# Sums of weight blocks in a Strassen MLP: VectorE adds or accumulating transfers

## The chip, the cores and the metric

The kernel runs on one core of a Trainium2 chip. The metric is the device time of one execution in microseconds. A core has TensorE (PE; matmuls), VectorE (DVE), ScalarE (ACT), GpSimd (POOL) and SyncE (SP), whose queue here only issues transfers. PE, DVE, ACT, POOL and SP each work through a row of instructions of their own, in order.

## What is computed

One residual block: a mixer sub-layer (a gated recurrence beside differential attention), then an MLP. Only the MLP is touched. It works on 512 positions of 1024 features, with 4096 hidden ones:

```python
h2 = rms_norm(x) * (1.0 + scale2) + shift2
ff = jnp.square(jax.nn.relu(h2 @ w_ff1[l])) @ w_ff2[l]
x = x + gate2 * ff
```

`scale2`, `shift2` and `gate2` come from a product with `w_ada` (adaLN).

## The kernel before

The numbers are float32. A matrix is split into a high and a low part (`wh`, `wl`; `p_0h`, `p_0l`): ACT casts the high part, DVE subtracts it to get the low one, and `mm3` (L131 to L133) multiplies high by high and high by low both ways, in three matmuls.

The MLP runs in four quarters (`qd` 0 to 3) of 1024 hidden features each. In a quarter, `hidden` computes eight blocks of 128 hidden features: each loads 512 KB of `w_ff1` (`load_w`, L120, three buffers with tag "w"), splits it (L124 on ACT, L125 on DVE, two buffers each) and runs 24 matmuls `f`, of 512 columns. In quarters 1 and 2 four of these blocks each also load a row of `w_ada` into a "w" buffer (L189) and reduce it on DVE (L190). Then `out_product` multiplies the quarter's 512 x 1024 activations by a 1024 x 1024 block of `w_ff2` with seven products p1 to p7, 24 matmuls each, in place of eight (Strassen's method). The weight side of four of them is a sum of 512 x 512 blocks b_00, b_01, b_10, b_11: p5 needs t1 = b_00 + b_01, p6 needs t2 = t1 + b_11, p7 needs t3 = b_01 + b_11, p4 needs t4 = t2 + b_10. Blocks are loaded in halves of 512 KB (`load_b`, L894, eight buffers with tag "b"), and each half is split like a weight (`split_b`, L940 and L941), 128 x 1024 elements per instruction. The halves are named `p_0` and `p_1` in the rows, whatever the product. Between the products, `beside()` runs the first three hidden blocks of the next quarter.

In quarters 0 to 2 the sums are made by `sums` (L984): DVE adds block onto block in place, so that the four blocks and all the sums take eight buffers. In quarter 3 (`by_dma`) they are made by transfers: `load_b` first loads one block into a buffer by a plain transfer on SP's queue (L894), then POOL issues transfers that add further blocks onto it (L896), and for t4 onto t2 (L917). Each accumulating transfer waits until the one before it on the same buffer has landed. That takes twelve half-block loads, so some of the eight buffers are used twice within the quarter.

The Tile scheduler sets the order of each engine's row from priorities and its own estimate of time; `tc.high_priority` moves the splits and the sums ahead. SP and POOL wait in order, so that a transfer whose buffer is not free holds up those behind it.

The functions that the change touches:

Of the kernel before, what the change touches and what calls it, by code (L numbers as in the profile page):

```python
# [21 lines left out]
ALU = mybir.AluOpType  # L22
# [20 lines left out]
HP = 130  # L43
# [10 lines left out]
def build(tc, out, x, xT_in, c, pos, vecs, reps, ada, w_xr, w_xr7, w_qk, w_v, w_gr, w_gm, w_lru,  # L54
          w_pr, w_pa, w_out, w_ff1, w_ff2):
    nc = tc.nc
    from contextlib import ExitStack

    with ExitStack() as es:
# [14 lines left out]
        def t_(name, dt=F32, tag="t"):  # L74
            return (tmp if tag == "t" else mix).tile([P, S], dt, name=name, tag=tag,
                                                     bufs=dict(t=B_T, a=B_A, r=B_R)[tag])
# [4 lines left out]
        def bank(name, tag="mm", bufs=4, dt=F32):  # L81
            return psum.tile([P, S], dt, name=name, tag=tag, bufs=bufs)
# [700 lines left out]
        acc = t_("acc", tag="a")  # L783
# [97 lines left out]
        def out_product(qd, raw, beside):  # L881
# [3 lines left out]
            def src_b(k, c, hf):  # L885
                k0 = (4 * k + 2 * hf) * P
                return w_ff2[qd, 4 * c:4 * c + 4, :, k0:k0 + 2 * P].rearrange("n p f -> p n f")

            def load_b(name, *parts):

                res = []
                for hf in range(2):
                    b = ff.tile([P, 4, 2 * P], F32, name=f"b{qd}_{name}{hf}", tag="b", bufs=8)
                    nc.sync.dma_start(b, src_b(*parts[0], hf))  # L894
                    for p_ in parts[1:]:
                        nc.gpsimd.dma_start(b, src_b(*p_, hf), accum_op=ALU.add)  # L896
                    res.append(b)
                return res

            def get_b(k, c):  # L900
                if (k, c) not in B:
                    B[k, c] = load_b(f"{k}{c}", (k, c))
                return B[k, c]

            by_dma = qd == 3

            def b_sum(name, acc, k, c, *parts):

                if not by_dma:
                    sums(acc, get_b(k, c))
                    return acc
                if acc is None:
                    return load_b(name, *parts, (k, c))
                for hf, b in enumerate(acc):
                    nc.gpsimd.dma_start(b, src_b(k, c, hf), accum_op=ALU.add)  # L917
                return acc
# [28 lines left out]
            def add_c(r, c, ps, sign):  # L947
                for t in range(2):
                    dst = C[r][c][t]
                    if qd == 0 and (r, c, t) not in seen:  # L950
                        seen.add((r, c, t))
                        nc.scalar.activation(dst, ps[t], AF.Copy, scale=float(sign))
                    else:
                        nc.vector.tensor_tensor(dst, dst, ps[t], op=ALU.add if sign > 0 else ALU.subtract)

            def product(name, a, bs, ps, first):

                fs = [split_b(b, f"{name}_{qd}_{i}", i) for i, b in enumerate(bs)]
                for hf in range(2):
                    for t in range(2):  # L960
                        for kk in range(2):
                            k = 2 * hf + kk
                            ts = slice(t * P, (t + 1) * P)
                            mm3(ps[t], a[0][:, k, ts], a[1][:, k, ts], fs[hf][0][:, kk], fs[hf][1][:, kk],
                                first and k == 0, k == 3, not first)
# [12 lines left out]
                                                   op0=ALU.mult, op1=ALU.add)  # L978
                    nc.sync.dma_start(out[n][:, cols], x1[n][:, cols])

            def sums(dsts, srcs):
                with tc.high_priority(HP):
                    for d, s_ in zip(dsts, srcs):
                        nc.vector.tensor_tensor(d, d, s_, op=ALU.add)  # L984

            X = [bank(f"X{qd}_{t}", "sc", 2) for t in range(2)]
            b11 = get_b(0, 0)
            product("p1", split_a(A[0][0], "a11", 2), b11, X, True)
# [7 lines left out]
            def second():  # L996
                a12 = split_a(A[0][1], "a12", 2)
                Y = [bank(f"Y{qd}_{t}") for t in range(2)]
                product("p2", a12, get_b(1, 0), Y, True)
                add_c(0, 0, Y, 1)  # L1000

            if qd == 3:
                second()
            t1 = b_sum("t1", None if by_dma else b11, 0, 1, (0, 0))
            Z = [bank(f"Z{qd}_{t}") for t in range(2)]
            product("p5", s1, t1, Z, True)
            beside()
            with tc.high_priority(HP):
                nc.vector.tensor_tensor(sx, sx, A[0][0], op=ALU.subtract)
                s2 = split_a(sx, "s2")  # L1010
            add_c(1, 1, Z, 1)
            t2 = b_sum("t2", None if by_dma else t1, 1, 1, (0, 0), (0, 1))
            product("p6", s2, t2, X, False)
            beside()
            with tc.high_priority(HP):
# [4 lines left out]
            nc.vector.tensor_tensor(A[0][0], A[0][0], A[1][0], op=ALU.subtract)  # L1020
            s3 = split_a(A[0][0], "s3")
            add_c(0, 1, Z, 1)
            t3 = b_sum("t3", None if by_dma else get_b(0, 1), 1, 1, (0, 1))
            product("p7", s3, t3, X, False)
            add_c(1, 1, X, -1)
            if qd < 3:
# [33 lines left out]
        for qd in range(4):  # L1060
            raw = hidden(qd, ahead)
            ahead = []

            def beside():

                if qd < 3:
                    ahead.append(t_(f"ahead{qd + 1}_{len(ahead)}"))
                    hidden_relu(qd + 1, len(ahead) - 1, ahead[-1])

            beside()  # L1070
            out_product(qd, raw, beside)
# [66 lines left out]
```

## Time and profile before

| | us |
|---|---|
| median of 3 runs (lowest, highest) | 875.87 (875.49, 876.06) |
| the profiled execution | 875.72 |
| its span, first to last instruction | 873.8 |
| PE busy | 860.9 (99%) |
| DVE busy | 636.8 (73%) |
| ACT busy | 478.6 (55%) |
| POOL busy | 15.1 (2%) |

The profile is of one execution. Its span starts at 0; the MLP's first matmuls run at about 540 us, and quarter 0's first product at 589 us. A busy PE is not the same as a PE at its best pace, since matmuls are pipelined: their starts tell the pace. Times to landing of a transfer run from its issue to the semaphore that tells of its end.

### The profile page before, as it was taken

Reading aid. Unit: us, or ns where it says so; the run is one execution under the profiler, and the core shown is the slowest. Engines: PE = TensorE matmul, PEld = TensorE weight load, DVE = VectorE, ACT = ScalarE, POOL = GpSimd, SP = SyncE. Lnnn points to the kernel's source line nnn. Section 1 sums busy time; section 2 is a strip of 40 time slices with the busy share of each in tenths; the row PEclk is TensorE's granted clock in tenths of the full one; section 3 lists DMA queues with packets and bytes.
Section 4 is the critical chain, followed back from the end, with each engine's and each line's share of the span. In section 5 each row is a group of like instructions: output and inputs, shape, how many; then the busy total and the mean of one; then the engine's idle time right before and its main releaser. Section 6 shows DMA issues by size and latency. Waiting matters only on the chain.

```text
span 873.8 us, 11279 instructions
## 1 busy us (share of the span) xinstructions
PE 860.9 (99%) x4012; PEld 706.1 (81%) x4012; DVE 636.8 (73%) x1155; ACT 478.6 (55%) x844; POOL 15.1 (2%) x50
## 2 busy tenths in 40 slices
PE   6999999999999999999999999999999999999998
PEld 3888887877878888888888888888888888888887
DVE  6998995699759754685657556858766885876397
ACT  6672547997538654646843343747545544554461
POOL 1000000000000000000000000000000000002110
PEclk9999999999999999999999999999999999999999
DMA  8979425512264372238445432822641345139572
GB/s 315 371 242 331 149 97 136 135 67 73 85 157 124 116 196 77 92 95 198 135 154 180 132 121 78 272 85 72 193 156 62 128 161 169 49 124 236 121 121 96
DMA packets 64571, 128.91 MB, mean 148 GB/s; under 512 B 6146, under 2 KB 30850, under 8 KB 64516
## 3 DMA queue, kind: packets, MB, share of 16 engines
q1 hardware_dynamic: 59236, 122.97, 44.6%
q0 software_dynamic: 5280, 5.24, 3.9%
q8 instruction: 31, 0.51, 0.2%
q14 instruction: 24, 0.20, 0.1%
HBM read 113.51 MB, written 2.10 MB: 132 GB/s over the span
## 4 chain that ended last, share of the span: by engine, by line
PE 92%; DVE 5%; ACT 1%; DMA 1%; issue 1%; SPq 0%
PE f L133 6%; PE f L131 6%; PE f L132 6%; PE X L132 3%; PE X L131 3%; PE X L133 3%; PE qk L133 3%; PE qk L131 3%; PE qk L132 3%; PE gm L132 2%; PE gm L131 2%; PE gm L133 2%; PE sc L582 2%; PE po L614 2%; PE xr L131 2%; PE v L131 2%
## 5 line engine op out<-in xcount | busy, mean ns | idle before, releaser
L124 ACT CAST wh<-w 128x1024 fp32r<-128x1024 f32 (+1 forms) x113 | 117.9, 1044 | 198.5 <-issue 44.9
L125 DVE TENSOR_TENSOR wl<-w,wh 128x1024 fp32r<-128x1024 f32 (+1 forms) x113 | 136.9, 1212 | 70.3 <-ACT wh L124 66.7
L133 PE MATMUL f<-h2h,wl 128*128 128x512 f32 x240 | 93.5, 390 | 0.4 <-DVE wl L125 0.4
L132 PE MATMUL f<-h2l,wh 128*128 128x512 f32 x240 | 93.2, 389 | 0.0
L131 PE MATMUL f<-h2h,wh 128*128 128x512 f32 x240 | 92.8, 390 | 0.0
L133 PEld LDWEIGHTS f<-h2h,wl 128*128 128x128 f32 x240 | 45.1, 188 | 10.1 <-DVE wl L125 0.8
L131 PEld LDWEIGHTS f<-h2h,wh 128*128 128x128 f32 x240 | 45.1, 188 | 9.4
L132 PEld LDWEIGHTS f<-h2l,wh 128*128 128x128 f32 x240 | 45.1, 188 | 9.2
L132 PE MATMUL gm<-hl,wh 128*128 128x512 f32 x128 | 51.7, 404 | 0.0
L133 PE MATMUL gm<-hh,wl 128*128 128x512 f32 x128 | 50.9, 398 | 0.0
L131 PE MATMUL gm<-hh,wh 128*128 128x512 f32 x128 | 50.7, 396 | 0.0
L131 PE MATMUL qk<-wh,hh 128*128 128x512 f32 x128 | 50.6, 396 | 0.0
L133 PE MATMUL qk<-wh,hl 128*128 128x512 f32 x128 | 50.5, 394 | 0.0
L132 PE MATMUL qk<-wl,hh 128*128 128x512 f32 x128 | 50.4, 394 | 0.0
L941 DVE TENSOR_TENSOR p_1l<-b,p_1h 128x1024 fp32r<-128x1024 f32 x24 | 29.3, 1222 | 26.3 <-ACT p_1h L940 26.1
L589 ACT ACTIVATE e<-e,nm 128x128 f32<-128x128 f32 (+3 forms) x64 | 35.5, 557 | 15.5 <-DVE nm L587 15.3
L940 ACT CAST p_1h<-b 128x1024 fp32r<-128x1024 f32 x24 | 25.2, 1051 | 31.0 <-PE f L132 22.9
L587 DVE CUSTOM_DVE_ANT_0 e<-sc,mask 128x128 f32<-128x128 f32 (+3 forms) x64 | 29.8, 484 | 16.1 <-PE sc L582 16.0
L941 DVE TENSOR_TENSOR p_0l<-b,p_0h 128x1024 fp32r<-128x1024 f32 x24 | 29.3, 1221 | 15.0 <-ACT p_0h L940 15.0
L940 ACT CAST p_0h<-b 128x1024 fp32r<-128x1024 f32 x24 | 25.3, 1055 | 24.6 <-PE X L133 12.4
L984 DVE TENSOR_TENSOR b<-b,b 128x1024 f32<-128x1024 f32 x24 | 29.0, 1217 | 0.1
L190 DVE CUSTOM_DVE_ANT_0 ada<-ada,cb,bada 128x1024 f32<-128x1024 f32 x16 | 20.5, 1282 | 10.1 <-DMA ada<-in_ada 10.1
(436 smaller groups left out, 2233.9 us busy)
## 6 DMA issues: line engine op xcount, KB each, us to landing
ada<-in_ada SPq DMA_DIRECT2D x64, 256.0 KB, 5.8
w<-in_w_ff SPq DMA_DIRECT2D x32, 512.0 KB, 3.3
b<-in_w_ff SPq DMA_DIRECT2D x30, 512.0 KB, 4.1
w<-in_w_qk SPq DMA_DIRECT2D x16, 512.0 KB, 3.3
w<-in_w_gm SPq DMA_DIRECT2D x16, 512.0 KB, 3.5
ada<-in_ada SPq DMA_DIRECT2D x16, 512.0 KB, 3.4
b_t<-in_w_ff POOLq DMA_DIRECT2D x10, 512.0 KB, 6.7
w<-in_w_gr SPq DMA_DIRECT2D x8, 512.0 KB, 3.6
```

The costliest lines, as they stand in the source:

```text
L124: i_w = nc.scalar.copy(wh[:, :n], w[:, :n])
L125: nc.vector.tensor_tensor(wl[:, :n], w[:, :n], f32(wh)[:, :n], op=ALU.subtract)
L131: nc.tensor.matmul(ps, lh, rh, start=first, stop=False, skip_group_check=more)
L132: nc.tensor.matmul(ps, lh, rl, start=False, stop=False, skip_group_check=more)
L133: nc.tensor.matmul(ps, ll, rh, start=False, stop=last, skip_group_check=more)
L190: nc.vector.tensor_tensor_reduce(w, w, cb, 1.0, bada[:, col:col + 1], op0=ALU.mult, op1=ALU.add, accum_out=mod[:, col:col + 1])
L582: nc.tensor.matmul(ps[m][:, :nn], q[m][:, qc], k[m][r][:, :nn], start=r == 0, stop=r == 1)
L587: nc.vector.tensor_tensor_reduce(e[:, :n], ps[m][:, :n], mask[:, S - n:], 1.0, 1e30, op0=ALU.add, op1=ALU.min, accum_out=nm)
L589: nc.scalar.activation(e[:, :n], e[:, :n], AF.Exp, bias=nm, scale=-1.0, accum_out=sums[:, 2 * i + m:2 * i + m + 1])
L940: nc.scalar.copy(v4(wh), v)
L941: nc.vector.tensor_tensor(v4(wl), v, f32(v4(wh)), op=ALU.subtract)
L984: nc.vector.tensor_tensor(d, d, s_, op=ALU.add)
```

## The change

The condition `by_dma` goes, and with it `sums`: all four quarters now make t1, t2, t3 and t4 by transfers, in the way of quarter 3. Quarter 3 itself is unchanged, and so is everything ahead of the MLP.

```diff
-            by_dma = qd == 3
-
             def b_sum(name, acc, k, c, *parts):
 
-                if not by_dma:
-                    sums(acc, get_b(k, c))
-                    return acc
                 if acc is None:
                     return load_b(name, *parts, (k, c))
                 for hf, b in enumerate(acc):
...
-            def sums(dsts, srcs):
-                with tc.high_priority(HP):
-                    for d, s_ in zip(dsts, srcs):
-                        nc.vector.tensor_tensor(d, d, s_, op=ALU.add)
...
-            t1 = b_sum("t1", None if by_dma else b11, 0, 1, (0, 0))
+            t1 = b_sum("t1", None, 0, 1, (0, 0))
...
-            t2 = b_sum("t2", None if by_dma else t1, 1, 1, (0, 0), (0, 1))
+            t2 = b_sum("t2", None, 1, 1, (0, 0), (0, 1))
...
-            t3 = b_sum("t3", None if by_dma else get_b(0, 1), 1, 1, (0, 1))
+            t3 = b_sum("t3", None, 1, 1, (0, 1))
```

The rows of PE stand in the same order as before. On the other engines the order moves. In what follows, `b_000` is the first half of block b_00, `b_t` a half of t1, t2 or t3, and the four-digit numbers tell buffers apart.

DVE, at the turn from quarter 0 to quarter 1, before:

```order
L954 TENSOR_TENSOR C_5557<-C_5557,Y_1_6098 128x512
L984 TENSOR_TENSOR b_000_6394<-b_000_6394,b_010_6447 128x1024
L125 TENSOR_TENSOR wl_6185<-w_6182,wh_6184 128x1024
L984 TENSOR_TENSOR b_010_6447<-b_010_6447,b_110_6527 128x1024
L941 TENSOR_TENSOR p_1_0l<-b_000_6394,p_1_0h 128x1024
L984 TENSOR_TENSOR b_000_6394<-b_000_6394,b_110_6527 128x1024
L125 TENSOR_TENSOR wl_6218<-w_6215,wh_6217 128x1024
L190 ISA ada_6284,mod<-ada_6284,cb,bada 128x1024
L190 ISA mod 128x1
L125 TENSOR_TENSOR wl_6254<-w_6251,wh_6253 128x1024
```

and now:

```order
L947 TENSOR_TENSOR C_5557<-C_5557,Y_1_6108 128x512
L125 TENSOR_TENSOR wl_6195<-w_6192,wh_6194 128x1024
L934 TENSOR_TENSOR p_1_0l<-b_t_6457,p_1_0h 128x1024
L190 ISA ada_6294,mod<-ada_6294,cb,bada 128x1024
L190 ISA mod 128x1
L125 TENSOR_TENSOR wl_6228<-w_6225,wh_6227 128x1024
L125 TENSOR_TENSOR wl_6264<-w_6261,wh_6263 128x1024
```

The three adds are gone, and the split of the fifth hidden block's weights (`wl_6218`, now `wl_6228`), which stood ahead of the reduction of the quarter's second adaLN row (`ada_6284`, now `ada_6294`), stands behind it. Quarter 2 has the same two in the same new order.

SP, in quarter 1, before:

```order
L894 DMA b_010_6447<-in_w_ff 128x4x256
L894 DMA b_011_6449<-in_w_ff 128x4x256
L894 DMA b_110_6527<-in_w_ff 128x4x256
L894 DMA b_111_6529<-in_w_ff 128x4x256
L894 DMA b_100_6688<-in_w_ff 128x4x256
L894 DMA b_101_6690<-in_w_ff 128x4x256
L189 DMA ada_6284<-in_ada 128x1024
L120 DMA w_6287<-in_w_ff 128x1024
```

and now:

```order
L894 DMA b_t_6457<-in_w_ff 128x4x256
L894 DMA b_t_6460<-in_w_ff 128x4x256
L894 DMA b_t_6537<-in_w_ff 128x4x256
L894 DMA b_t_6541<-in_w_ff 128x4x256
L894 DMA b_110_6617<-in_w_ff 128x4x256
L894 DMA b_111_6619<-in_w_ff 128x4x256
L894 DMA b_t_6660<-in_w_ff 128x4x256
L189 DMA ada_6294<-in_ada 128x1024
L894 DMA b_t_6663<-in_w_ff 128x4x256
L120 DMA w_6297<-in_w_ff 128x1024
```

Six loads of blocks have become eight; the second adaLN row's load stands behind the load of t3's first half, and the load of t3's second half stands ahead of the next weight load.

POOL, quarters 0 and 1, now (before, POOL had no transfer ahead of quarter 3):

```order
L896 DMA b_t_5938<-in_w_ff 128x4x256
L896 DMA b_t_5942<-in_w_ff 128x4x256
L896 DMA b_t_5938<-in_w_ff 128x4x256
L896 DMA b_t_5942<-in_w_ff 128x4x256
L896 DMA b_t_6061<-in_w_ff 128x4x256
L896 DMA b_t_6064<-in_w_ff 128x4x256
L910 DMA b_t_5938<-in_w_ff 128x4x256
L910 DMA b_t_5942<-in_w_ff 128x4x256
L896 DMA b_t_6457<-in_w_ff 128x4x256
L896 DMA b_t_6460<-in_w_ff 128x4x256
L896 DMA b_t_6537<-in_w_ff 128x4x256 x2
L896 DMA b_t_6541<-in_w_ff 128x4x256 x2
```

In quarter 0 both halves of t2 (`b_t_5938`, `b_t_5942`) get their first addition before either gets its second; from quarter 1 on a half gets both in a row (`x2`), so that POOL waits for a landing between them. t4's additions (L910) stand ahead of the next quarter's t1.

## Rows read from the trace of the kernel before

**Rows 1.** The page, sections 1 and 4: busy us and share; the chain by engine.

```profile
PE 860.9 (99%) x4012; PEld 706.1 (81%) x4012; DVE 636.8 (73%) x1155; ACT 478.6 (55%) x844; POOL 15.1 (2%) x50
...
PE 92%; DVE 5%; ACT 1%; DMA 1%; issue 1%; SPq 0%
```

**Rows 2.** Stretches, 562.2 to 861.1 us: length, busy us by engine, clock, DMA share.

```profile
589.10:643.50 54.40, 54.40 (x242) 45.06 (x241) 43.24 (x44) 31.01 (x39) 0.00 (x0) 1.00 0.40 127
...
sum 298.90, PE 298.90 PEld 247.53 DVE 214.43 ACT 152.81 POOL 12.86; mean PE 42.70 PEld 35.36 DVE 30.63 ACT 21.83 POOL 1.84
```

**Rows 3.** Waits of TensorE, 540 to 861 us: total, times, longest.

```profile
PE f L133 <- DVE wl L125: 0.4, 1, 0.4
```

**Rows 4.** Timeline of TensorE near 562, 573, 644 us: start, us, instruction, idle before.

```profile
561.22 0.39 PE L131 MATMUL f<-h2h,wh 128*128 128x512 f32 x1
561.45 0.39 PE L132 MATMUL f<-h2l,wh 128*128 128x512 f32 x1
562.20 0.50 PE L133 MATMUL f<-h2h,wl 128*128 128x512 f32 x1 [0.36 <-DVE wl L125]
...
573.22 0.39 PE L133 MATMUL f<-h2h,wl 128*128 128x512 f32 x1
...
643.94 0.39 PE L133 MATMUL f<-h2h,wl 128*128 128x512 f32 x1
```

**Rows 5.** Line 984, the removed adds: ns min/median/max, first and last start.

```profile
L984 DVE TENSOR_TENSOR b<-b,b x24: 1212/1216/1226, 562.1 to 768.7; 128x1024 f32<-128x1024 f32 x24
```

**Rows 6.** Line 896, issues on POOL: ns min/median/max.

```profile
L896 POOL DMA_DIRECT2D b_t<-in_w_ff x8: 1264/1277/1412, 789.2 to 837.4; - x8
```

**Rows 7.** POOL's transfers issued at 789.19, 797.94, 799.62, 809.02, 843.43: last column, us to landing.

```profile
b_t<-in_w_ff POOLq DMA_DIRECT2D x1, 512.0 KB, 8.4
...
b_t<-in_w_ff POOLq DMA_DIRECT2D x1, 512.0 KB, 10.8
...
b_t<-in_w_ff POOLq DMA_DIRECT2D x1, 512.0 KB, 14.0
...
b_t<-in_w_ff POOLq DMA_DIRECT2D x1, 512.0 KB, 7.3
...
b_t<-in_w_ff POOLq DMA_DIRECT2D x1, 512.0 KB, 6.0
```

**Rows 8.** SP's transfers issued at 553.74, 554.83, 635.89, 790.18, 793.20, 798.35.

```profile
b<-in_w_ff SPq DMA_DIRECT2D x1, 512.0 KB, 6.3
...
b<-in_w_ff SPq DMA_DIRECT2D x1, 512.0 KB, 8.2
...
ada<-in_ada SPq DMA_DIRECT2D x1, 512.0 KB, 3.2
...
b_t<-in_w_ff SPq DMA_DIRECT2D x1, 512.0 KB, 7.2
...
b_t<-in_w_ff SPq DMA_DIRECT2D x1, 512.0 KB, 5.9
...
w<-in_w_ff SPq DMA_DIRECT2D x1, 512.0 KB, 8.2
```

**Rows 9.** Timeline of ACT, quarter 0: casts for t1's and t2's first halves.

```profile
564.88 1.05 ACT L940 CAST p_0h<-b 128x1024 fp32r<-128x1024 f32 x1
...
592.00 1.06 ACT L940 CAST p_0h<-b 128x1024 fp32r<-128x1024 f32 x1 [0.36 <-PE X L133]
```

**Rows 10.** Timeline of VectorE, quarter 0 and the start of quarter 1.

```profile
567.10 0.69 DVE L145 TENSOR_TENSOR a11l<-r,a11h 128x512 fp32r<-128x512 f32 x1
...
631.17 1.22 DVE L941 TENSOR_TENSOR p_0l<-b,p_0h 128x1024 fp32r<-128x1024 f32 x1 [1.20 <-ACT p_0h L940]
...
634.65 1.22 DVE L125 TENSOR_TENSOR wl<-w,wh 128x1024 fp32r<-128x1024 f32 x1
...
639.38 1.23 DVE L125 TENSOR_TENSOR wl<-w,wh 128x1024 fp32r<-128x1024 f32 x1
640.52 1.27 DVE L190 CUSTOM_DVE_ANT_0 ada<-ada,cb,bada 128x1024 f32<-128x1024 f32 x1
```

## The prediction

> **What bounds the kernel now.** The page's first section comes first: TensorE is busy for 860.9 of 873.8 us, VectorE for 636.8, and the chain of work that ended last runs 92% over TensorE [rows 1]. A busy share can hide a lagging engine, so the next view is the table of stretches over the MLP. In the stretch from 562.2 to 861.1 us TensorE is busy for 298.90 of 298.90 us at a granted clock of 1.00 (2.4 GHz) [rows 2]. The waits of TensorE between 540 and 861 us are one line: 0.4 us, once, for `wl` on VectorE [rows 3]. The matmuls around it show its price: starts are 0.23 us apart, then one comes 0.75 us after the last, at 562.20, which is 0.5 us lost [rows 4]. All 24 adds that the change removes lie between 562.1 and 768.7 us, and stand on VectorE beside this unbroken row of matmuls [rows 5]. The reader should see here that the MLP has 0.5 us to win on TensorE, and that the question is whether something new makes TensorE wait.
>
> **The change part by part.** The order of matmuls stays the same row by row. The sum is made against the profiled execution, 875.72 us: its span of 873.8 and 1.9 around it, beside a median of 875.87 (875.49 to 876.06).
>
> *Removed from VectorE:* 24 adds of 1.216 us, 29.2 us [rows 5]. They lie wholly beside TensorE's work. The one stall at 562.20 waits for a split whose place in VectorE's order has no removed add ahead of it, so it stays. Gain: 0; at most the 0.5 us.
>
> *Added transfers:* in each of quarters 0 to 2, four more plain 512 KB loads on SP's queue (12 instead of 8) and ten accumulating ones on POOL's. Plain loads that queue up land 1.5 us apart (553.74 + 6.3 = 560.0 and, two later, 554.83 + 8.2 = 563.0) [rows 8]; accumulating ones that queue up without company 2.7 us apart (799.62 + 14.0 = 813.6, 809.02 + 7.3 = 816.3) [rows 7]. A quarter with adaLN rows would then ask for 24 x 1.5 + 10 x 2.7 = 63 us of transfers, and it lasts 360 matmuls of 0.227 us, 81.6 us. The transfers fit on average; before, the DMA share there is 0.40 [rows 2]. What counts is when single ones land. POOL does nothing else, and its issues take 1.26 to 1.41 us [rows 6].
>
> *Place A, quarter 0, t1's first half.* It was the first of the adds, at 562.1 [rows 5]; now it is a plain load and then an accumulating one, and the cast `p_0h` that reads it stands in ACT's row ahead of the split of the weights for the hidden block that starts at 572.76. The plain load is the one ahead of that issued at 553.74, so it lands 1.5 us before 560.0, at 558.5. An accumulating transfer takes 6.0 us to land alone, 8.4 when it is first in POOL's queue and plain loads run beside it, 10.8 and 14.0 when it stands behind other accumulating ones [rows 7]. This one is first in its queue with four loads still under way, so I take 8.4: it lands at 566.9, where the cast now starts at 564.88 [rows 9]. The limit: the cast 1.05, then on VectorE its low half 1.14, two `a11l` of 0.6 and the split `wl` of 1.22 make 4.6 us [rows 9, 10], and the third matmul of the block, at 573.22 [rows 4], needs that `wl`; so it may land at 568.6. That leaves 1.7 us. Cost 0; with the ends 6.0 and 14.0 it is 0 and 4.0 us.
>
> A rule of the Trainium skill says less for the same transfer: "DMA: Bandwidth & Descriptors", section "Anatomy of one DMA — SWDGE (gpsimd) path", fits 2.0 us plus the bytes over 436 GB/s, an estimate of 3.2 us for 512 KB. The rows have 6.0 alone. By the page the half would land at 561.7 with 6.9 us to spare, by the rows at 566.9 with 1.7; the sum is 0 by either, and the rows decide how near it is.
>
> *Quarter 0, t2*, two accumulating transfers on each half. From 797.6 to 813.6 us three steps of the queue took 5.3 us each [rows 7]. So t1's second half lands at 572, t2's first pass at 577.5 and 583, its second at 588 and 593.5. The cast that reads the first of these starts at 592.00 now [rows 9], the other one later. Hidden, with 4 us to spare. t3 and t4 come later than that and are read later still.
>
> *Place B, quarters 1 and 2.* Here the order of VectorE changes. Before, the split `wl` for the fifth hidden block stood ahead of the reduction of the second adaLN row (L190); now it stands behind it. TensorE needs that split at 643.94 in quarter 1 [rows 4], so the reduction, 1.27 with 1.21 to the next, and the split, 1.23 [rows 10], must start by 641.45: that is the limit for the landing of the adaLN row. It is issued when the `wl` ahead is done: that one starts at 634.65 [rows 10] behind an add that is gone, so it ends at about 635.1 instead of 635.9. Alone the row landed 3.2 us after its issue [rows 8], which would be 638.3. A weight load on the same queue behind loads of `b` with accumulating transfers beside took 8.2 [rows 8], which would be 643.3, 1.85 us too late. Nearer to the case: the transfer ahead of it on SP's queue is t3's load, which needs the buffer that the split at 631.17 [rows 10] frees, so it is issued at 632.4; loads beside accumulating transfers landed 5.9 and 7.2 us after issue [rows 8], so it lands between 638.3 and 639.6, and the adaLN row 1.5 later, 639.8 to 641.1. In quarter 3 three accumulating transfers were issued in the 9.2 us ahead of that weight load, the last at 797.94; here t1's two and t2's first spread over 17 us, since POOL then waits for t2's first pass to land. I take 640.5, 0.9 us before the limit. Cost 0; ends 0 and 1.85 us, in each of quarters 1 and 2 (81.6 us later the same chain stands again).
>
> *Queues passed:* SP waits in order, and the load for t3's second half waits for p5's first split in quarters 1 and 2, with the next weight load behind it. That split ends by about 638, and the weight load's own buffer comes free only behind the `wl` that starts at 639.38 [rows 10], so that wait costs nothing. But this `wl` now ends near 643 instead of 640.6 by the working above, and the weight load and the third adaLN row go out then; at 8.2 they land at 651.2, the row's reduction, an `a11l` and the `wl` behind it take 3.0, and TensorE needs that `wl` two blocks after 643.94, at 654.8. Hidden by 0.6 us. On POOL t4's transfers wait for p6's splits and the next quarter's t1 stands behind them; t1's buffers come free later than that anyway. *Quarter 3 and the tail* keep their rows.
>
> Sum: 875.72 + 0 (adds) + 0 (A) + 0 (B twice) = 875.7, in the middle of the three runs before; with their spread I forecast 875.9.
>
> **The rivals.**
>
> *Slower: the adaLN row lands behind the new traffic (place B).* Plain and accumulating transfers take each other's time: a `b` load took 7.2 us where the adaLN row alone took 3.2 [rows 8]. The margin is 0.9 us in an estimate that adds three transfers, and the wait falls straight on TensorE, which has no slack to take it back: the blocks behind it follow without a gap. It decides once the row takes over 6.35 us from issue to landing. At 8.2 it gives 1.85 us twice, 879.4; with 10.8 for A in place of 8.4 another 0.7, 880.1. Against it: the accumulating transfers lie wider than in quarter 3, and quarter 3 already runs all of them with TensorE fully occupied. A stall of under 1.75 us in all, the part of it that no measurement tells, is likelier than the full one.
>
> *Faster: VectorE's 29.2 us matter.* This would need TensorE to wait for VectorE. The rows leave 0.5 us, so 875.2 is the best, and this lies within 0.2%. A gain beyond that would need a pace of matmuls under 0.227 us; nothing in the profile points to one.
>
> *The change does nothing of what it says.* The 24 adds are gone from VectorE's row and 30 transfers stand on POOL's, so only the accumulation could be cheaper than quarter 3 shows: 875.7.
>
> **How the numbers follow.** A measurement of this kernel tells 0.2%, 1.75 us, from no change. No stall: 0.55, 875.4 to 876.2. A stall of under 1.75 us in A and B together: 0.21, 876.2 to 877.6. More than that: 0.20, 877.6 to 880.1. Gain over 1.75 us: 0.04, 873.9. So faster 0.04, within 0.2% 0.76, slower 0.20. The range runs from 875.3 to 879.0: it takes in one full stall and half of the second, and leaves about 0.1 above and 0.06 below.
>
> **What would show it.** VectorE's busy time falls by about 29 us to 608. TensorE stays busy for the whole of 562 to 861 us, and its waits remain one line of 0.4. In quarter 0 the cast `p_0h` of t1 starts near 566.9 after a wait for a DMA on `b_t`; over 568.6 would show on the block that starts at 572.76. In quarters 1 and 2 the second adaLN row lands about 5.4 us after issue, and VectorE waits for it ahead of L190. The forecast is wrong if TensorE's waits name `wl` at about 644 and 725.5 us, or `wh` or `wl` at 572.8; each such wait is its own price, and their sum the difference in the span. If none is there and the time still moves, the pace of the matmuls has changed, which this account has not foreseen.

## The result and the profile after

| | before | after |
|---|---|---|
| median (lowest, highest), us | 875.96 (875.49, 876.22), 4 runs | 881.38 (878.57, 882.59), 4 runs |
| ratio, 95% interval | | 1.0058 [1.0046, 1.0071] |
| the profiled execution, us | 875.72 | 881.36 |
| its span, us | 873.8 | 879.4 |

The changed kernel is 0.6% slower, above the range of the prediction (875.3 to 879.0); the sign is that of its rival "slower". Its runs also lie 4.0 us apart, those of before 0.7.

The page of after, sections 1, 3 and 4: busy time, queues (packets, MB, share of 16 DMA engines), and the chain by engine.

```profile
PE 861.5 (98%) x4012; PEld 705.6 (80%) x4012; DVE 611.2 (69%) x1131; ACT 478.6 (54%) x844; POOL 53.6 (6%) x80
...
q1 hardware_dynamic: 65572, 129.26, 46.0%
q0 software_dynamic: 21120, 20.97, 15.4%
...
PE 82%; DVE 10%; DMA 3%; ACT 2%; issue 1%; SPq 1%; DVEq 0%; ACTq 0%
```

VectorE lost its 24 adds and 25.6 us of busy time against [rows 1]. The adds' durations sum to 29.2, which the prediction expected; instructions that follow each other there overlap a little (by 0.09 us at 640.52 in [rows 10]), so that an add fills less than its duration. TensorE's busy time is what it was. The chain, 92% TensorE before, now crosses to VectorE, ScalarE and transfers. The stretch from 562.2 to 861.1 us of after (columns as in [rows 2]):

```profile
562.20:861.10 298.90, 295.07 (x1299) 243.38 (x1298) 185.92 (x201) 152.36 (x191) 50.11 (x40) 1.00 0.86 203
```

TensorE is busy for 295.07 of 298.90 us at the same granted clock of 1.00, where it was busy throughout [rows 2]. So the matmuls have not slowed; TensorE waits. Its waits between 540 and 880 us in after (total, times, longest), against the one of 0.4 us in [rows 3]:

```profile
PE f L133 <- DVE wl L125: 2.6, 3, 1.3
PE f L131 <- ACT wh L124: 1.3, 1, 1.3
```

Where they stand is told by the same matmuls in both traces, since TensorE's row is the same. After:

```profile
562.61 0.50 PE L133 MATMUL f<-h2h,wl 128*128 128x512 f32 x1 [0.37 <-DVE wl L125]
...
574.59 0.50 PE L131 MATMUL f<-h2h,wh 128*128 128x512 f32 x1 [1.26 <-ACT wh L124]
574.92 0.40 PE L132 MATMUL f<-h2l,wh 128*128 128x512 f32 x1
576.21 0.50 PE L133 MATMUL f<-h2h,wl 128*128 128x512 f32 x1 [0.89 <-DVE wl L125]
576.54 0.40 PE L131 MATMUL f<-h2h,wh 128*128 128x512 f32 x1
...
730.14 0.50 PE L133 MATMUL f<-h2h,wl 128*128 128x512 f32 x1 [1.32 <-DVE wl L125]
730.48 0.40 PE L131 MATMUL f<-h2h,wh 128*128 128x512 f32 x1
...
875.24 0.28 PE L133 MATMUL pl<-a22h,pl_1l 128*128 128x256 f32 x1
```

and before, the partners of the lines at 576.54, 730.48 and 875.24:

```profile
573.44 0.39 PE L131 MATMUL f<-h2h,wh 128*128 128x512 f32 x1
...
725.76 0.39 PE L131 MATMUL f<-h2h,wh 128*128 128x512 f32 x1
...
870.42 0.28 PE L133 MATMUL pl<-a22h,pl_1l 128*128 128x256 f32 x1
```

After runs behind before by 0.41 us at 562 (ahead of the change), by 3.10 behind the first hidden block, by 4.72 behind the block in quarter 2, by 4.82 at the last matmul, and by 5.6 at the end of the span. The 5.6 us are thus 0.4 that were there already, **2.7 at place A**, **1.6 at place B of quarter 2**, 0.1 between, and 0.8 in the tail. Place B of quarter 1 cost nothing in this execution. A wait costs more than its idle time: the three new ones are idle for 3.47 us (1.26, 0.89, 1.32) and cost 4.3, some 0.3 more each.

Place A in after, first on ACT, then on VectorE:

```profile
571.50 1.05 ACT L933 CAST p_0h<-b_t 128x1024 fp32r<-128x1024 f32 x1 [6.12 <-DMA b_t<-in_w_ff]
...
573.50 1.04 ACT L124 CAST wh<-w 128x1024 fp32r<-128x1024 f32 x1
```

```profile
572.59 1.22 DVE L934 TENSOR_TENSOR p_0l<-b_t,p_0h 128x1024 fp32r<-128x1024 f32 x1 [8.48 <-ACT p_0h L933]
...
574.93 1.22 DVE L125 TENSOR_TENSOR wl<-w,wh 128x1024 fp32r<-128x1024 f32 x1
```

The cast of t1's first half, which started at 564.88 [rows 9], waits 6.12 us for the accumulating transfer. `wh` and `wl` of the next hidden block stand behind it on ACT and on VectorE, and TensorE waits for each in turn. Place B on VectorE in after, quarter 1 and quarter 2:

```profile
644.11 1.28 DVE L190 CUSTOM_DVE_ANT_0 ada<-ada,cb,bada 128x1024 f32<-128x1024 f32 x1 [3.15 <-DMA ada<-in_ada]
...
645.32 1.22 DVE L125 TENSOR_TENSOR wl<-w,wh 128x1024 fp32r<-128x1024 f32 x1
...
727.65 1.28 DVE L190 CUSTOM_DVE_ANT_0 ada<-ada,cb,bada 128x1024 f32<-128x1024 f32 x1 [3.90 <-DMA ada<-in_ada]
...
728.86 2.36 DVE L125 TENSOR_TENSOR wl<-w,wh 128x1024 fp32r<-128x1024 f32 x2
```

In both, VectorE waits for the adaLN row with a split behind it. The transfers that all this hangs on, issued at 560.95 (t1's first half), 638.26 and 719.86 (the rows); the last column is us to landing:

```profile
b_t<-in_w_ff POOLq DMA_DIRECT2D x1, 512.0 KB, 10.5
...
ada<-in_ada SPq DMA_DIRECT2D x1, 512.0 KB, 5.7
...
ada<-in_ada SPq DMA_DIRECT2D x1, 512.0 KB, 7.7
```

### The profile page after: what moved, and what is told of

It is laid out like the page before. It is cut to its first block, busy times and chain, and to the rows that moved or that the text cites. A ratio compares the mean times of both kernels' runs of the same rounds, so it can differ in the third digit from the quotient of the medians.

```text
span 879.4 us, 11373 instructions
## 1 busy us (share of the span) xinstructions
PE 861.5 (98%) x4012; PEld 705.6 (80%) x4012; DVE 611.2 (69%) x1131; ACT 478.6 (54%) x844; POOL 53.6 (6%) x80
## 3 DMA queue, kind: packets, MB, share of 16 engines
q1 hardware_dynamic: 65572, 129.26, 46.0%
q0 software_dynamic: 21120, 20.97, 15.4%
## 4 chain that ended last, share of the span: by engine, by line
PE 82%; DVE 10%; DMA 3%; ACT 2%; issue 1%; SPq 1%; DVEq 0%; ACTq 0%
PE f L133 5%; PE f L131 5%; PE f L132 5%; PE X L132 3%; PE X L131 3%; PE X L133 3%; PE gm L132 2%; PE gm L131 2%; PE gm L133 2%; DVE wl L125 2%; PE qk L133 2%; PE qk L131 2%; PE qk L132 2%; DMA b_t<-in_w_ff 2%; PE sc L582 2%; PE po L614 2%
## 5 line engine op out<-in xcount | busy, mean ns | idle before, releaser
L896 POOL DMA_DIRECT2D b_t<-in_w_ff x32 | 41.2, 1500 | 719.3 <-DMA b_t<-in_w_ff 673.7
L934 DVE TENSOR_TENSOR p_0l<-b_t,p_0h 128x1024 fp32r<-128x1024 f32 x15 | 18.3, 1222 | 18.4 <-ACT p_0h L933 18.4
L133 PEld LDWEIGHTS qk<-wh,hl 128*128 128x128 f32 x128 | 24.1, 188 | 4.7
L132 PEld LDWEIGHTS qk<-wl,hh 128*128 128x128 f32 x128 | 24.1, 189 | 4.6
L131 PEld LDWEIGHTS qk<-wh,hh 128*128 128x128 f32 x128 | 24.2, 189 | 4.5
```

Source lines behind the costliest of these rows:

```text
L131: nc.tensor.matmul(ps, lh, rh, start=first, stop=False, skip_group_check=more)
L132: nc.tensor.matmul(ps, lh, rl, start=False, stop=False, skip_group_check=more)
L133: nc.tensor.matmul(ps, ll, rh, start=False, stop=last, skip_group_check=more)
L934: nc.vector.tensor_tensor(v4(wl), v, f32(v4(wh)), op=ALU.subtract)
```

## The experiments

Three groups of runs shared their runs of before: medians 875.85 (21 runs), 876.10 (33) and 876.07 (26). Each result is the median of 5 to 11 runs and the ratio to before with its interval.

**By quarter.** Sums by transfers in quarter 0 alone (`q0_only`) or in quarters 1 and 2 alone (`q12_only`), beside quarter 3; the rest by `sums` as before.

```diff
-            by_dma = qd == 3
+            by_dma = qd in (0, 3)
...
-            by_dma = qd == 3
+            by_dma = qd > 0
```

> Sums by transfers in quarter 0 (and, as before, in quarter 3); quarters 1 and 2 keep VectorE's adds, and VectorE's row there is that of before. Theory (two places: A, t1's first half lands too late in quarter 0; B, the split of the fifth hidden block waits behind the second adaLN row in quarters 1 and 2): A stays, about 2.5 us lost at the hidden block that starts near 573 us, B is gone; with 0.4 to 0.8 us that I have not placed, 878.4 to 879.3. Rival (30 more transfers slow everything a little, a third in each of three quarters): 5.4 / 3 = 1.8, so 877.8, and no single stall of over 1 us.

> Sums by transfers in quarters 1, 2 and 3; quarter 0 keeps VectorE's adds. Theory of the two places: no wait at 573 us; a wait of TensorE for wl at the fifth hidden block of quarter 2 (near 726 us) and perhaps of quarter 1 (near 644), 0 to 2 us each, its size that of the adaLN row's landing over 6.35 us; about 877.4, between 876 and 879. Rival (a little everywhere): 879.5.

Measured: 876.79, 1.0012 [1.0003, 1.0021], and 877.72, 1.0030 [1.0018, 1.0042]. The two add up to 2.8 of 5.4 us. What makes the other 2.6 is not settled: the profiled execution of after lost 2.4 us more at A than that of `q0_only`, and 0.4 more in the tail than both together, but a profile is one execution of each kernel. "A little everywhere" falls for `q12_only`: TensorE waits there for `wl` at one place of quarter 2 and nowhere else beyond the old 0.4.

```profile
726.39 0.50 PE L133 MATMUL f<-h2h,wl 128*128 128x512 f32 x1 [1.03 <-DVE wl L125]
```

For `q0_only` my number was too high. Its profiled execution, the fastest of its eleven, loses only 0.3 us at A: the accumulating transfer is as slow as in after (10.2 us), but it was issued at 558.00, not at 560.95, since the plain load that POOL waits for landed 3 us sooner (the semaphore of its landing is complete at 557.12, in after at 560.08). Only 0.9 of that is the earlier MLP (the old stall of 562.61 stands at 561.70 there). The same cast as above:

```profile
568.20 1.05 ACT L938 CAST p_0h<-b_t 128x1024 fp32r<-128x1024 f32 x1 [3.72 <-DMA b_t<-in_w_ff]
```

So place A costs from 0.3 to 2.7 us in the two executions that were profiled. The median of `q0_only` is 0.9 above before, and 0.3 of that can be its tail (3.7 us from the last matmul to the end, 3.4 before). That the runs of these kernels lie further apart than those of before fits this, though the slower runs themselves left no trace to see it in.

**A alone taken away.** All sums by transfers but t1 of quarter 0 (`t1_q0_dve`).

```diff
-            t1 = b_sum("t1", None, 0, 1, (0, 0))
+            if qd == 0:
+                t1 = b11
+                sums(t1, get_b(0, 1))
+            else:
+                t1 = b_sum("t1", None, 0, 1, (0, 0))
```

> The changed kernel, but t1 of quarter 0 alone is made by two adds of VectorE, as before; all other sums by transfers. Theory of the two places: A is gone (no wait at 573 us), B stays as in the changed kernel: 878 to 879.3. If t2's first pass, which is now first in POOL's queue, were also late, a wait would show near 592 us or later. Rival (a little everywhere): 28 of 30 transfers are left, 881.

Measured: 879.11, 1.0040 [1.0028, 1.0052], 2.3 us under after, though the two intervals overlap. What the trace shows is that the wait at 573 is gone. Two waits for `wl` are left:

```profile
661.10 0.50 PE L133 MATMUL f<-h2h,wl 128*128 128x512 f32 x1 [0.96 <-DVE wl L125]
...
727.69 0.50 PE L133 MATMUL f<-h2h,wl 128*128 128x512 f32 x1 [0.99 <-DVE wl L125]
```

The second is place B in quarter 2. The first is one that no theory named: place C, the fourth adaLN row of quarter 1, again with a split behind its reduction. That order is not new: in before the reductions of the third and fourth rows already stand ahead of their splits, as here the fourth and its split:

```profile
652.03 1.29 DVE L190 CUSTOM_DVE_ANT_0 ada<-ada,cb,bada 128x1024 f32<-128x1024 f32 x1 [0.82 <-DMA ada<-in_ada]
...
655.42 1.23 DVE L125 TENSOR_TENSOR wl<-w,wh 128x1024 fp32r<-128x1024 f32 x1 [2.10 <-ACT wh L124]
```

**The size of the packets.** The same kernel with `w_ff2` laid out so that each half block is 4 KB in a row for a partition, not four rows of 1 KB (`packets`). SP's plain loads of blocks get the larger rows, too.

```diff
-                k0 = (4 * k + 2 * hf) * P
-                return w_ff2[qd, 4 * c:4 * c + 4, :, k0:k0 + 2 * P].rearrange("n p f -> p n f")
+                return w_ff2[qd, k, c, hf].rearrange("p (n f) -> p n f", n=4)
...
```

> The changed kernel, with w_ff2 laid out so that a half block is 4 KB in a row for each partition, in place of four rows of 1 KB; every instruction and order is the same. Theory (t1's accumulating transfer is slow since it gets one packet of 1 KB for each packet of 4 KB of the weight loads beside it): its first landing comes in 8 us or less in place of 10.5, the stalls at 573 us go, and the time falls by about 2.5 us to 878 to 879; the adaLN row then meets larger packets of the accumulating transfers and may land later, B up to 2 us in each quarter. Rival (an accumulating transfer is slow by itself, in its start and in the adding): 10 to 11 us to landing, and 881.

Measured: 884.53, 1.0098 [1.0079, 1.0117], not the 878 to 879 expected. At A nothing waits at 573: t1's first half lands in 8.5 us. But it was also issued 1.9 us sooner, at 559.03. By the limit of the prediction, 568.6 and 0.5 for an MLP that runs later here, either gain alone would have left it some 0.5 us late (559.03 + 10.5, or 560.95 + 8.5; an estimate), so this run does not show that the packets alone cure A. What they do shows in four microseconds in which both queues have work beside the weight loads, 566.5 to 570.5 us, first in after, then here (packets, MB, share):

```profile
q1 hardware_dynamic: 248, 0.95, 62.9%
q0 software_dynamic: 317, 0.31, 48.4%
```

```profile
q0 software_dynamic: 153, 0.56, 70.2%
q1 hardware_dynamic: 147, 0.54, 36.1%
```

POOL's queue (q0) moves 0.56 MB in place of 0.31, and SP's (q1) 0.54 in place of 0.95. The packets stay near one to one (153 to 147 here), and where both queues have rows of 1 KB, from 571.5 to 575.5 us of after, they are equal:

```profile
q0 software_dynamic: 480, 0.48, 73.6%
q1 hardware_dynamic: 480, 0.48, 43.9%
```

The Trainium skill ("DMA: Bandwidth & Descriptors", section "Queues, rings and completion order") says that each DMA engine takes its queues in turn, a packet at a time; these counts agree. A queue with rows of 1 KB beside one with rows of 4 KB thus gets the smaller part of the bytes, here 0.31 of 1.26 MB.

The price comes back at place C. The fourth row's load is issued when the third's buffer is free, at 652.26, and its reduction starts at 661.03; TensorE waits there in both quarters.

```profile
661.03 1.28 DVE L190 CUSTOM_DVE_ANT_0 ada<-ada,cb,bada 128x1024 f32<-128x1024 f32 x1 [7.06 <-DMA ada<-in_ada]
```

```profile
663.52 0.50 PE L133 MATMUL f<-h2h,wl 128*128 128x512 f32 x1 [2.59 <-DVE wl L125]
...
748.54 0.50 PE L133 MATMUL f<-h2h,wl 128*128 128x512 f32 x1 [2.97 <-DVE wl L125]
```

**Order without traffic, traffic without order.** Place B has two ingredients. `order_before` is the kernel before with only the reduction put ahead of the split; `no_accum12` is `q12_only` with the new order and the plain loads but without the accumulating transfers of quarters 1 and 2; `rows_behind` is `t1_q0_dve` with all 28 transfers and the reductions of the second, third and fourth rows behind the splits. `no_accum12` thus leaves out parts of its sums. In the diffs `after(x, y)` puts x behind y on its engine.

```diff
+                    after(wl4, i_ada)
...
-                    for p_ in parts[1:]:
+                    for p_ in parts[1:] if qd == 3 else ():
...
+                    if n >= 5:
+                        after(i_ada, wl4 if n == 5 else last_wl[0])
```

> The kernel before with one thing of the change: in quarters 1 and 2 the reduction of the second adaLN row is put ahead of the split of the fifth hidden block, as it stands in the changed kernel; the adds stay on VectorE, no new transfer. Theory (the order costs only because the traffic delays the row): the row lands about 3.2 us after its issue, so no wait at 644 and 726 us; 875.9 within 0.5. Rival (the order alone costs): a wait of 1 us or more at both places, 878 or more.

> The kernel with transfers in quarters 1 to 3 and VectorE's adds in quarter 0, but in quarters 1 and 2 the 20 accumulating transfers are left out (so the sums there lack their second and third blocks); every other instruction and order is the same, and the 12 plain loads stay. Theory (accumulating transfers delay the adaLN row): the row lands in 4 to 5.5 us and the wait at 726 us goes; 875.9, at most 876.5, in place of 877.7. Rival (the four more plain loads delay it): the wait stays, 877.5.

> The kernel with t1 of quarter 0 on VectorE and all other sums by transfers; in quarters 1 and 2 the reductions of the second, third and fourth adaLN rows are put behind the split of the weights that they stood ahead of. All 28 transfers stay. Theory (the whole cost there is VectorE waiting for a row with a split behind it): no wait of TensorE over 0.5 us in quarters 1 and 2, 875.9 to 876.4 in place of 879.1. Rival (the transfers cost by themselves, or the weight loads are as late as the rows): 877.5 to 879, with waits for wh or wl that stand behind a weight load.

| quarters 1 and 2 | no accumulating transfers | accumulating transfers |
|---|---|---|
| split ahead of the reduction | before: 1 | `rows_behind`: 1.0010 [1.0002, 1.0019] |
| reduction ahead of the split | `order_before`: 1.0000 [0.9990, 1.0009]; `no_accum12`: 0.9998 [0.9989, 1.0007] | `q12_only`: 1.0030 [1.0018, 1.0042]; `t1_q0_dve`: 1.0040 [1.0028, 1.0052] |

Neither ingredient costs anything by itself in TensorE's waits. But the table is clean for the second row alone: `rows_behind` also turns the third and fourth rows, which stand ahead of their splits in before, so the traffic in the very order of before was not run, and place C could show in it. In `order_before` the second row of quarter 2 lands in 3.3 us, and the split behind it is in time; in `rows_behind` it takes 7.5 us, as late as in after, and VectorE has the split behind it already, so its wait holds up nothing:

```profile
720.95 1.23 DVE L126 TENSOR_TENSOR wl<-w,wh 128x1024 fp32r<-128x1024 f32 x1 [0.30 <-ACT wh L125]
724.44 1.29 DVE L192 CUSTOM_DVE_ANT_0 ada<-ada,cb,bada 128x1024 f32<-128x1024 f32 x1 [2.27 <-DMA ada<-in_ada]
```

`rows_behind` has TensorE busy for 298.88 of 298.90 us from 562.2 to 861.1. `no_accum12` settles the rival "faster" too: VectorE has none of its 16 adds in quarters 1 and 2, no transfer does them instead, and the time does not move.

**All of it mended.** The changed kernel with the reductions behind the splits and, in quarter 0, t1's loads ahead of those of b_00 (`early_rows`).

```diff
+            if qd == 0:
+                t1 = b_sum("t1", None, 0, 1, (0, 0))
             b11 = get_b(0, 0)
...
-            t1 = b_sum("t1", None, 0, 1, (0, 0))
+            if qd > 0:
+                t1 = b_sum("t1", None, 0, 1, (0, 0))
```

> The changed kernel, all sums by transfers, with two moves: the rows' reductions behind the splits as in the run before, and in quarter 0 t1's two plain loads ahead of those of b_00, so that its accumulating transfers go out about 3 us earlier. Theory of the places: t1's first half lands near 565 although its accumulating transfer still takes 9 to 11 us, the cast of it starts by 568 and nothing waits at 573; 875.9 to 876.5. Rival (the cost is in the traffic): 878 or more. If b_00, which now loads later, is late, a wait shows at 560 to 563 us.

Measured: 877.66, 1.0020 [1.0011, 1.0030], 3.7 us under after, above the 876.5 I expected. The accumulating transfer took 11.5 us, but was issued at 553.26, and the cast waits for nothing:

```profile
565.33 1.04 ACT L939 CAST p_0h<-b_t 128x1024 fp32r<-128x1024 f32 x1
```

In the profiled execution (876.77, one of the fastest) TensorE waits 0.5 us in all. What its median has above that is not explained.

**The tail.** `rows_behind` is 0.7 us slower than before, although its last matmul starts at 870.44, as before (870.42): its span is 874.7, so the loss lies behind that. I took the count of transfers on SP's queue for the cause and added four small loads, to before and to `rows_behind`; a third kernel joins all remedies, larger packets with them.

```diff
+            if qd == 3:
+                for i in range(4):
+                    nc.sync.dma_start(ff.tile([P, 4], F32, name=f"pad{i}", tag="pad", bufs=4), vecs[:, :4])
```

> The kernel before with four loads of 2 KB more on SP's queue in quarter 0, which nothing reads, so that it issues 366 transfers, as many as the kernel with transfers in quarter 0 alone. The kernels that issue 366 or 374 transfers on SP's queue end 3.7 to 4.3 us after the start of the last matmul, those with 362 or 370 end 3.4 us after it; their last stores land on other semaphores of the eight that take turns. Theory (the tail depends on the count of transfers modulo eight): 3.7 to 4.3 us from the last matmul to the end, 876.4 to 877. Rival (the tail grows with the accumulating transfers): 3.4 us and 876.0.

> The kernel with t1 of quarter 0 on VectorE, the other sums by transfers and the rows' reductions behind the splits, with four loads of 2 KB more on SP's queue: 378 transfers, the same place in the turn of eight as the kernel before. Theory (of the 0.7 us that this kernel lost without a stall of TensorE the tail is all): 3.4 us from the last matmul to the end and 876.0 to 876.2, the time of before. Rival (the tail grows with the accumulating transfers): 4.2 us and 876.8.

> All sums by transfers, none on VectorE: the changed kernel with half blocks in rows of 4 KB, the rows' reductions behind the splits, and the four small loads. Theory (place A goes by the larger packets, the places behind the rows by the order): t1's first half lands in 8 to 9 us, no wait of TensorE over 0.6 us, and 876.0 to 876.8 in place of 884.5. Rival (with larger packets the accumulating transfers crowd out the weight loads, which took 10 to 16 us there in quarter 0): waits for wh or wl behind weight loads, over 878.

Measured: 876.15, 1.0000 [0.9990, 1.0009]; 876.82, 1.0008 [0.9999, 1.0017]; 877.33, 1.0013 [1.0005, 1.0022]. The times are those of the rival (876.0 and 876.8). The count does move the tail in the traces: from the last matmul to the end it is 3.4 us in before and 3.7 in `before_plus4`, 4.3 in `rows_behind` and 3.7 in `rows_behind_plus4` (the theory said 3.4 there); in the medians that does not show, and intervals of 0.1% to either side would hide 0.3 us. The last two stores, together, land in a median of 1.8 us in before, 1.9 in `q12_only` and `before_plus4`, 2.2 in `rows_behind_plus4` and 2.4 in after. So the count is at most a part, and why the stores land later behind 28 or 30 added transfers stays open; it is 0.3 to 0.8 us from the last matmul to the end. The third kernel is above the 876.0 to 876.8 expected. It has TensorE waiting for 0.4 us in all in its profiled execution, 876.23, which is the fastest of its eleven; the others reach 878.47, and what they lost was not seen. None of the versions beats the kernel before.

## Why the prediction was wrong

*The removed adds: 0.* Right. They lay beside TensorE's work, and `no_accum12` shows that their absence moves nothing. The 0.5 us at 562.20 stayed, too.

*Place A: the mechanism was right, two terms of the sum were too small.* The step that failed is "so I take 8.4". It was the row of quarter 3 that looked nearest; here the transfer took 10.5, 10.2 and 11.5 us in three kernels, and 8.5 with 4 KB packets. That a transfer is first in POOL's queue does not tell its time: t2's first pass, first in that queue in `t1_q0_dve` and `rows_behind`, took 8.6 and 10.0. The fit of the Trainium skill ("DMA: Bandwidth & Descriptors", section "Anatomy of one DMA — SWDGE (gpsimd) path"), an estimate of 3.2 us, was further off still. The other term is the start. I put the landing of the plain load at 558.5, which is what before has (558.49 by its semaphore); in after it was 560.08, and POOL's transfer went out 0.87 us behind it, a time that the sum left out. Against a slack of 1.7 us, 2.1 more to landing and 2.0 more at the start (560.95 less 558.5 and less the 0.4 of the later MLP) make 2.4, where 2.7 was measured. The same plain load landed at 557.12 in `q0_only`: a slack that is smaller than what one such load varies by is no slack.

*t2 in quarter 0.* Hidden, as predicted; the second passes landed at 591.44 and 594.54, where 588 and 593.5 were forecast. No wait stands there.

*Place B in quarter 1: right.* The row landed in 5.7 us, 5.4 was forecast, and no wait followed. *In quarter 2* the step that failed is "81.6 us later the same chain stands again": the row took 7.65 us. POOL's queue stands otherwise there. Its transfers issued at 711.94 and 713.34 landed at 720.29 and 724.75, beside the row, where in quarter 1 the last one landed at 640.82 and the next was issued at 641.10. While the row was under way (638.3 to 644.0 and 719.9 to 727.5 us) POOL's queue moved 0.11 MB in quarter 1 and 0.30 MB in quarter 2:

```profile
q0 software_dynamic: 119, 0.11, 11.6%
...
q0 software_dynamic: 312, 0.30, 25.5%
```

The threshold of the rival, 6.35 us from issue to landing, held: 7.65 less 6.35 is 1.30, and TensorE was idle for 1.32, which cost 1.6. That it comes this close is in part luck, since its terms are estimates to some tenths. "Each such wait is its own price" was too low by the 0.3 us per wait.

*The third row, "hidden by 0.6 us".* No wait in after, but this chain was followed one row too short. The fourth row is issued only when the third's buffer is free, and it is that one that stalled TensorE in `t1_q0_dve` and in `packets`.

*The rivals and the chances.* "Slower by B" had the mechanism, its threshold and, with A at 10.8, a time of 880.1; it got 0.20. What I weighed wrongly were margins of 0.6, 0.9 and 1.7 us, the first two of them twice, each taken as hidden, although each was a difference of estimated landings, and landings differ by 2 us and more between rows of the same kind. That one of them would fail, and by more than a little, was far likelier than that. "Against it", that quarter 3 ran all transfers without a wait, was no argument: no adaLN rows are loaded there. The tail of 0.8 us was not foreseen at all.

## What to carry to other kernels

VectorE's time beside a full TensorE was worth nothing here, but moving it to transfers put other transfers at risk: before such a change, list what stands in order behind each wait for a transfer, since every new wait of TensorE here came from a split queued behind an instruction that waited for a late one. Order took these waits away (`rows_behind`, `early_rows`), though not the 0.7 us and more that stayed above before; larger packets moved the wait elsewhere. A margin worked out from landings is to be held against the spread of landings in the trace, and all margins together, not one by one.

## What the runs showed of the hardware

- An accumulating transfer of 512 KB with rows of 1 KB, first in POOL's queue beside plain loads, took 8.0 to 11.5 us from issue to landing: 10.5, 10.2 and 11.5 for t1's first half, 8.6, 10.0 and 8.0 for t2's in `t1_q0_dve`, `rows_behind` and `rows_behind_plus4`. With rows of 4 KB t1's took 8.5 and 8.7 (`packets_rows_plus4`). The one of 6.0 us in [rows 7], called alone, stood behind another, issued at 840.55; one with nothing else on POOL's queue took 5.6 (`t1_q0_dve`, issued at 603.19).
- In after POOL's queue moves nothing up to 563.5 us for the one issued at 560.95.
- Accumulating holds the DMA engines longer: for 480 packets of 1 KB each, 73.6% of their time against 43.9% for plain ones; over the whole of after, 15.4% for 20.97 MB against 46.0% for 129.26 MB, twice as much per byte.
- Queued accumulating transfers landed 4.4 us apart beside plain loads in after (571.48, 575.94, 580.38, 584.74), between the 2.7 and the 5.3 that the prediction used.
- Packets of two queues with work went near one to one, so the rows' size set each queue's share: larger rows gave POOL's queue 0.56 MB in place of 0.31 and SP's 0.54 in place of 0.95 in four microseconds, and `packets` has 2.6 and 3.0 us of waiting at C.
